# A depthwise convolution as column-tiled tap steps on shifted copies, layer norm beside gate blocks, and earlier w_out loads, in one decoder layer

## The chip, the cores and the metric

The kernel runs on all 8 cores of one Trainium2 chip as one program. The time is the device time of the slowest core in microseconds (us). Some executions fall in a second, slower state: the cores of one die (cores 0 to 3, or 4 to 7) show a lower granted TensorE clock and the time is some per cent longer. The profile of a run shows one execution and, where no core is named, its slowest core. In the views of this document PE is TensorE matmul, PEld its weight load, DVE VectorE, ACT ScalarE, POOL GpSimd and SP SyncE; "SPq" is the queue on which SyncE issues DMA transfers. Every operation passes through one helper, so all lines read L212 and a group is told by its tiles and its form.

## The reference, cut to what matters

The reference is one layer of a decoder. The change touches its middle: a gated linear unit (GLU), a 31-tap depthwise convolution over 1024 channels, a layer norm over the channels, two sigmoid gates, and the product with `w_out`. Attention runs before it and a SwiGLU feed-forward network (FFN) after it; neither is changed.

```python
def conv_branch(u, u_past, w_dw, b_dw, ln_g, ln_b, w_pw, b_pw):
    uc = jnp.concatenate([u_past, u], axis=1)
    y = lax.conv_general_dilated(uc, w_dw[:, None, :], window_strides=(1,), padding='VALID', ...,
                                 feature_group_count=D_CONV) + b_dw      # D_CONV = 1024, 31 taps
    y = jax.nn.silu(layer_norm(y, ln_g, ln_b))
    return y @ w_pw + b_pw, uc[:, -(CONV_WIDTH - 1):]

# in decoder_layer:
    glu = z[..., :o1] + b_glu
    u = glu[..., :D_CONV] * jax.nn.sigmoid(glu[..., D_CONV:])
    gate_conv = jax.nn.sigmoid(z[..., o4:o5])
    gate_attn = jax.nn.sigmoid(z[..., o5:])
    conv_out, new_conv = conv_branch(u, u_past, ...)
    attn_out = o_att.reshape(N, L, ATT_OUT) @ w_o_att
    x = x + (gate_conv * conv_out + gate_attn * attn_out) @ w_out
    # ... FFN
```

Each core holds 1024 prompt rows and 16 sample rows. The 1024 channels are worked in 8 blocks of 128 channels, one per partition.

## The kernel before

The operations are listed in program order for each engine, and a helper adds the semaphore waits that the data needs. So the place of a line in the listing fixes its place on its own engine. The GLU and the convolution of a block follow one another at once. A depthwise convolution becomes a matmul by putting each tap on a diagonal: 31 diagonal 128x128 matrices `dg`, each multiplied with a moving window that is shifted by one column.

```python
for ph in range(4):                              # two channel blocks per weight load
    for n4 in range(2):
        n = 2 * ph + n4; ui = n % 2
        for ti, (c0, nc_) in enumerate(TG3):     # columns 357, 357, 356
            # 16 + 16 matmuls: value half and gate half of the GLU; then
            # ACT: sg = sigmoid(gate half); DVE: ubb[ui] or u2 = (value half + bias) * sg
            ...
            if ti == 0:                          # 31 diagonal weight matrices
                S.op('dve', lambda e: e.tensor_tensor(out=dg[ui], in0=mkap(identb, [[0, 31], [1, 128]]), in1=..., op=ALU.mult))
        S.op('pe', lambda e: e.transpose(out=PS[4][0:46, 0:128], in_=u2[:, 310:356], identity=identf))
        for j in range(31):
            S.op('pe', lambda e: e.matmul(PS[2][:, :], lhsT=dg[ui][:, j, :], rhs=ubb[ui][:, j:j + 512], ...))
            S.op('pe', lambda e: e.matmul(PS[3][:, :], lhsT=dg[ui][:, j, :], rhs=ubb[ui][:, 512 + j:512 + j + 512], ...))
            S.op('pe', lambda e: e.matmul(PS[6][:, 0:16]..., lhsT=dg[ui][:, j, :], rhs=ucb[ui][:, :, j:j + 4], ...))  # samples
        ...
```

The layer norm then sums over the channels with a matrix of ones in fp32, block by block, and VectorE and ScalarE apply it. Only after that come the 48 mix blocks (16 output blocks of 128, three column groups each), and only after those the loads of `w_out`.

```python
for ti, (hf, a, nc_, c0) in enumerate(TGL):      # four column groups of 256 or 264
    for n in range(8):
        S.op('pe', lambda e: e.matmul(PS[b0][:, 0:nc_], lhsT=onesf, rhs=yv, start=(n == 0), stop=(n == 7)))
        S.op('act', lambda e: e.activation(out=ysq[qi][:, 0:nc_], in_=yv, func=AF.Square))
        S.op('pe', lambda e: e.matmul(PS[b1][:, 0:nc_], lhsT=onesf, rhs=ysq[qi][:, 0:nc_], start=(n == 0), stop=(n == 7)))
# mean, rstd, then per group and block: DVE subtract, DVE multiply, ACT Silu -> cT
...
for jh in range(8):
    # per mix block: 16 + 16 gate matmuls, 8 with w_pw, 4 with w_o; ACT: two sigmoids; DVE: three ops -> mixT
    ...
wo = [load_out(c) for c in range(4)]             # w_out in four quarters
for t in range(8):
    S.dma('sp', xacc[t], xext[1024 + 128 * t:1024 + 128 * (t + 1), :])
```

The softmax here doesn't subtract the row's maximum and nothing guards it: scores larger than these inputs give would overflow.

## Time and profile before

The median is 2339.89 us over 4 executions (2337.38 to 2629.14; the longest was slow).

The page of the profile opens with the busy shares, the busy tenths of PE and the granted clock in 40 slices of the span, and the chain of work that ended last, by engine:

```profile
span 2349.9 us, 34317 instructions; the slowest of 8 cores (2316.9 to 2349.9 us)
PE 2138.1 (91%) x13248; PEld 1247.2 (53%) x13248; DVE 816.0 (35%) x1418; ACT 367.5 (16%) x712; POOL 125.2 (5%) x129
...
PE   3697799798899978999958989999999999999997
...
PEclk9898899899999998999989999999999999999987
...
PE 85%; DMA 8%; DVE 3%; ACT 2%; issue 2%; another core or an unknown queue 1%; SPq 0%; DVEq 0%; ACTq 0%; POOLq 0%
```

TensorE bounds the kernel: it is 91% busy and makes up 85% of the chain. Only work taken from PE, or idle time of PE filled, can shorten it. The low digit in the row "PE" (a 5, in the 21st slice) is the wait for `w_out` at about 1210 us.

The stages on core 5, each from the start of its first matmul (read from PE's timeline):

| stage | starts at, us | lasts, us |
|---|---|---|
| GLU, convolution, layer norm statistics | 568.0 | 295.1 |
| layer norm applied, 48 mix blocks | 863.1 | 342.3 |
| product with w_out | 1205.5 | 160.7 |
| FFN, to the end | 1366.1 | 983.8 |

The PE timeline of the kernel before, core 5. The columns are start, duration, engine, line, operation, then the output with the moving input and the weights, the shape of the weights, the shape of the moving input, type and count; in brackets the idle time before it and what ended it.

```profile
617.75 14.72 PE L212 MATMUL ps<-t_55,t_52 128*128 128x357 bf16 x96
634.07 0.27 PE L212 MATMUL ps<-t_43,t_112 128*46 128x128 f32 x1 [1.60 <-DVE t_112 L212]
...
648.68 14.72 PE L212 MATMUL ps<-t_55,t_53 128*128 128x357 bf16 x96
...
834.26 0.68 PE L212 MATMUL ps<-yA,t_45 128*128 128x256 f32 x2
...
882.51 0.45 PE L212 MATMUL ps<-t_120,t_54 128*128 128x347 bf16 x1 [14.52 <-ACT t_120 L212]
...
904.51 4.77 PE L212 MATMUL ps<-t_55,t_52 128*128 128x346 bf16 x16 [6.65 <-ACT t_135 L212]
...
1205.45 3.62 PE L212 MATMUL ps<-wf_146,t_134 128*128 128x512 bf16 x16
1240.82 5.18 PE L212 MATMUL ps<-wf_143,t_134 128*128 128x512 bf16 x16 [31.75 <-DMA wf_143<-w_out]
```

One block is 14.72 us of GLU matmuls, 1.60 us idle for the transpose, and 14.5 us of convolution (from 634.18 to 648.68). The statistics take 28.8 us (834.26 to 863.1). The mix stage then waits for the layer norm, in steps of 14.52 and 6.65 us among others: it lasts 342.3 us, where 48 blocks at 6.49 us are 311.5, so 30.8 us are lost. And the second quarter of `w_out` is 31.75 us late: its load was issued at 1202.2 us only. (The first quarter's, on a free buffer, was issued at 1129.5 us, since the POOL queue runs ahead of PE.)

One more reading matters: the attention stage of this same kernel already uses column tiles (weights of 128 rows by 32 columns). Three of them with different moving inputs start within 10 ns, and the next three begin 0.22 us later (the fourth line):

```profile
115.42 0.39 PE L212 MATMUL ps<-t_52,t_55 128*32 128x512 bf16 x1
115.42 0.39 PE L212 MATMUL ps<-t_53,t_55 128*32 128x512 bf16 x1
115.43 0.39 PE L212 MATMUL ps<-t_54,t_55 128*32 128x512 bf16 x1
115.65 0.38 PE L212 MATMUL ps<-t_52,t_55 128*32 128x512 bf16 x1
```

### The profile page before, as it was taken

The page shows a single profiled execution, that of the slowest core. Times are in us where ns is not written, and L with a number is a line of the kernel's source. Part 1 is how long each engine was busy: PE and PEld are TensorE (multiplying, and loading weights), DVE is VectorE, ACT ScalarE, POOL GpSimd, SP SyncE. Part 2 cuts the span into 40 slices and gives each one's busy share as a digit, 9 for nine tenths or more (in the row PEclk, how much of TensorE's full clock was granted, in tenths as well). Part 3 has the DMA queues.
Part 4 walks back from the last instruction along what each step waited for, and adds up shares of the span by engine and source line. Part 5 has one row for each costly group of instructions (what it writes and reads, how often), then busy time and mean ns, then how long its engine had stood idle before and what let it go on. Part 6 is the DMA issues. An engine that isn't in the chain of part 4 may idle for free.

```text
span 2349.9 us, 34317 instructions; the slowest of 8 cores (2316.9 to 2349.9 us)
## 1 busy us (share of the span) xinstructions
PE 2138.1 (91%) x13248; PEld 1247.2 (53%) x13248; DVE 816.0 (35%) x1418; ACT 367.5 (16%) x712; POOL 125.2 (5%) x129
## 2 busy tenths in 40 slices
PE   3697799798899978999958989999999999999997
PEld 2354354465455554666633555665565565565653
DVE  2543375464222214222211424224324314414125
ACT  3451121111011143111100320000000000000012
POOL 0000000000000100010000010000000000010000
PEclk9898899899999998999989999999999999999987
DMA  8847678756500072555656589987989895554303
GB/s 196 192 94 111 99 174 167 149 149 122 96 1 1 10 93 27 73 79 71 86 128 149 72 151 149 185 126 140 168 127 160 143 148 85 90 79 76 62 21 126
DMA packets 217971, 256.93 MB, mean 109 GB/s; under 512 B 6626, under 2 KB 186082, under 8 KB 212540
## 3 DMA queue, kind: packets, MB, share of 16 engines
q0 software_dynamic: 185808, 127.93, 39.9%
q1 hardware_dynamic: 30468, 82.96, 12.5%
q10 hardware_dynamic: 1536, 43.85, 7.8%
q8 instruction: 108, 1.77, 0.3%
q14 instruction: 51, 0.42, 0.1%
HBM read 366.61 MB, written 60.30 MB: 182 GB/s over the span
## 4 chain that ended last, share of the span: by engine, by line
PE 85%; DMA 8%; DVE 3%; ACT 2%; issue 2%; another core or an unknown queue 1%; SPq 0%; DVEq 0%; ACTq 0%; POOLq 0%
PE ps L212 85%; DMA wf_143<-w_out 2%; DMA t_52<-w_in 1%; DMA t_58<-xext 1%; DMA t_69<-cv 1%; DMA t_67<-sqkv 1%; DMA t_63<-ck 1%; DMA t_64<-ck 1%; DVE t_133 L212 0%; DVE t_132 L212 0%; DMA t_59<-xext 0%; DMA t_105<-state 0%; ACT t_60 L212 0%; ACT t_172 L212 0%
## 5 line engine op out<-in xcount | busy, mean ns | idle before, releaser
L212 PE MATMUL ps<-t_55,t_52 128*128 128x347 bf16 (+3 forms) x1152 | 188.6, 321 | 6.7 <-ACT t_135 L212 6.7
L212 PE MATMUL ps<-t_54,t_55 128*128 128x512 bf16 (+1 forms) x640 | 149.7, 388 | 14.9 <-DMA t_54<-w_in 14.9
L212 PEld LDWEIGHTS ps<-t_55,t_52 128*128 128x128 bf16 x1152 | 115.4, 100 | 70.6 <-issue 7.0
L212 PE MATMUL ps<-t_53,t_55 128*128 128x512 bf16 (+1 forms) x640 | 146.6, 383 | 5.2 <-DVE t_55 L212 5.2
L212 PE MATMUL ps<-t_55,t_53 128*128 128x347 bf16 (+3 forms) x960 | 150.8, 312 | 0.0
L212 PEld LDWEIGHTS ps<-t_55,t_53 128*128 128x128 bf16 x960 | 93.9, 98 | 48.8
L212 PE MATMUL ps<-t_52,t_55 128*128 128x512 bf16 (+1 forms) x432 | 109.1, 411 | 7.0 <-DMA t_52<-w_in 6.9
L212 ACT ACTIVATE t_170<-ps 128x347 f32<-128x347 f32 (+1 forms) x66 | 30.4, 460 | 542.4 <-PE ps L212 542.4
L212 PEld LDWEIGHTS ps<-t_54,t_55 128*128 128x128 bf16 (+1 forms) x640 | 76.0, 122 | 70.6 <-issue 23.7
L212 PEld LDWEIGHTS ps<-t_53,t_55 128*128 128x128 bf16 (+1 forms) x640 | 75.1, 122 | 60.1 <-issue 11.4
L212 PE MATMUL ps<-t_134,wh_152 128*128 128x347 bf16 (+1 forms) x576 | 93.9, 318 | 0.0
L212 PE MATMUL ps<-t_134,wh_151 128*128 128x347 bf16 (+1 forms) x576 | 93.9, 318 | 0.0
L212 PE MATMUL ps<-t_134,wh_153 128*128 128x347 bf16 (+1 forms) x576 | 93.1, 316 | 0.5 <-DVE t_134 L212 0.5
L212 PE MATMUL ps<-t_134,wh_154 128*128 128x347 bf16 (+1 forms) x576 | 90.9, 311 | 0.0
L212 PE MATMUL ps<-t_120,t_54 128*128 128x347 bf16 (+1 forms) x384 | 66.7, 314 | 17.4 <-ACT t_120 L212 17.4
L212 PE MATMUL ps<-t_134,wh_150 128*128 128x347 bf16 (+1 forms) x480 | 77.9, 317 | 0.0
L212 PE MATMUL ps<-t_134,wh_149 128*128 128x347 bf16 (+1 forms) x480 | 77.7, 317 | 0.0
L212 PEld LDWEIGHTS ps<-t_52,t_55 128*128 128x128 bf16 (+1 forms) x432 | 43.6, 105 | 60.6 <-issue 23.8
L212 PE MATMUL ps<-t_134,wh_147 128*128 128x347 bf16 (+1 forms) x480 | 75.7, 311 | 0.0
L212 PE MATMUL ps<-t_134,wh_148 128*128 128x347 bf16 (+1 forms) x480 | 75.7, 311 | 0.0
L212 ACT ACTIVATE t_171<-ps 128x347 f32<-128x347 f32 (+1 forms) x66 | 30.4, 460 | 283.7 <-PE ps L212 283.7
L212 PEld LDWEIGHTS ps<-t_134,wh_151 128*128 128x128 bf16 x576 | 57.4, 100 | 31.0
(379 smaller groups left out, 3079.9 us busy)
## 6 DMA issues: line engine op xcount, KB each, us to landing
t_52<-w_in POOLq DMA_DIRECT2D x12, 1024.0 KB, 10.4
t_53<-w_in POOLq DMA_DIRECT2D x10, 1024.0 KB, 12.5
t_58<-xext SPq DMA_DIRECT2D x8, 1024.0 KB
t_59<-xext SPq DMA_DIRECT2D x8, 1024.0 KB, 7.5
kso<-ck ACTq DMA_DIRECT2D x8, 1016.0 KB, 10.7
vso<-cv ACTq DMA_DIRECT2D x8, 1016.0 KB, 10.9
t_52<-w_in POOLq DMA_DIRECT2D x3, 2048.0 KB, 25.0
wh_153<-w_gate POOLq DMA_DIRECT2D x6, 1024.0 KB, 9.9
```

The lines of the kernel that those rows point to most:

```text
L212: self.q[eng].append(lambda e: getattr(e, meth)(*a, **kw).then_inc(s, 1))
```

## The change

The change has three parts.

1. **Convolution in four column tiles.** A diagonal 128x128 matrix uses one row in 128 for each output. In its place the kernel handles 32 channels per column tile, with the four quarters of the 128 partitions holding the same 32 channels shifted by 0, 8, 16 and 24 columns. One matmul then does four taps for 32 channels, and eight steps `a` do 32 taps (the last is zero). The four tiles `g` work side by side. The price is the shifted data: 16 copies from `ubb` to `U4` for each block, each of 32 partitions and 1032 columns, on the SP queue. The convolution of block n-1 is placed inside block n, after its second column group, so that PE has something to do while the copies run. The sample rows are convolved on VectorE.
2. **Layer norm beside gate blocks.** VectorE and ScalarE add up the values and the squares over the 8 blocks as they come, so that the ones-matmuls are needed once. The sigmoids become tanh, whose results are kept for the first nine gate blocks (`ND = 9`); PE runs those while the layer norm is applied, and the nine mixes are done afterwards.
3. **Two of four w_out loads start in the mix stage**, after blocks 35 and 41.

The diff, cut to its core:

```diff
+        def conv_in(n):
+            i_ = n % 2
+            S.op('dve', lambda e: e.tensor_tensor(out=dgc[i_], ...))          # 32 small diagonals
+            for g in range(4):
+                for i in range(4):
+                    S.dma('sp', U4[i_][32 * i:32 * i + 32, g, :], ubb[i_][32 * g:32 * g + 32, 8 * i:8 * i + 1032])
+
+        def conv(n):
+            i_ = n % 2
+            for hf in range(2):
+                for a in range(8):
+                    for g in range(4):
+                        S.op('pe', lambda e: e.matmul(PS[4 + hf][32 * g:32 * g + 32, :], lhsT=dgc[i_][:, 4 * a + g, :], rhs=U4[i_][:, g, a + 512 * hf:a + 512 * hf + 512], start=(a == 0), stop=(a == 7)))
+                S.op('act', ...)                                               # + bias -> yv[n]
 ...                                             # in block n, after column group ti
-                for j in range(31):
-                    ... three matmuls with dg[ui][:, j, :] ...
+                if ti == 1 and n > 0:
+                    conv(n - 1)
+                    conv_sample(n - 1)
+                    stat_add(n - 1)
+            S.op('act', lambda e: e.copy(out=ubb[ui][:, 714:1054], in_=u2[:, 0:340]))
+            conv_in(n)
+            ...
+            if n4 == 1:
+                if ph < 2:
+                    glu_load(ph + 2)             # weights of a later pair of blocks, on the POOL queue
+                else:
+                    gates_load(ph - 2)
 ...
-        a4_load(0)
-        a4_load(1)
-        ... statistics, layer norm, then the mix ...
+        gates_load(1)
+        gate(0)
+        rows_out(7)
+        gate(1)
+        conv(7)
+        ...
+        gate(2)
+        stat_mm(6, 0, 0, 512)
+        ...                                      # ln_rstd, ln_apply between gate(3) ... gate(8)
+        for it in range(48):
+            if it >= ND:
+                gate(it)
+            mix(it)
+            ...
+            if it == 35:
+                wo.append(load_out(0))
+            if it == 41:
+                wo.append(load_out(1))
 ...
-        wo = [load_out(c) for c in range(4)]
+        wo += [load_out(2), load_out(3)]
```

## The prediction

> **What bounds it now.** TensorE: 85% of the chain of waits, 91% busy, at a granted clock of 1.00 in every long stretch. The change touches 568 to 1241 us (PE timeline):
>
> - GLU and convolution, 568 to 834 us. One channel block: 14.7 us of GLU matmuls, 1.6 us idle for a transpose waiting on VectorE, 14.5 us of convolution (31 taps x 0.460 us). The first block also waits 9.6 us (state load, sample normalisation).
> - Layer norm, 834 to 905 us: 28.8 us of fp32 ones-matmuls, then about 30 us more than the mix needs, while ScalarE and VectorE normalise.
> - Mix, 48 blocks of 6.49 us, all PE. Then PE waits 31.8 us for a w_out load issued only at 1202 us; the next 16 matmuls take 5.2 instead of 3.6 us (cold clock).
>
> **Removed.** A convolution becomes 8 taps x 2 halves, each four 128x32 column tiles. This trace already has such tiles: three of 512 columns start together every 0.215 us, four of 256 every 0.108 us. That agrees with the Trainium skill, "TensorEngine Tiling (Array Packing)", Key Properties: tiles work in parallel. So 16 x 0.216 = 3.5 us instead of 14.5, and the 1.6 us bubble goes: 12.6 x 8 = 101 us. First block: 8 us. Statistics: 2080 fp32 columns x 1.69 ns = 3.5 instead of 28.8 us: 25 us. Layer norm beside nine gate blocks (9 x 4.7 = 42 us of PE; VectorE needs about 22 us to apply, 10 for statistics): 30 us. First two w_out loads 39 us and more before use (a load lands in 27): 32 us. Ideal sum, all PE: 196 us.
>
> **Given back.**
> 1. Each block needs 16 copies on the SP queue. SP issues one per about 0.5 us (eight xacc loads took 4.5 us), so 8 us, after 2 us of evacuation and before some 2.5 us of landing: 12.5 us after the GLU ends, while PE reaches the convolution after 9.8 us. PE stalls 2 to 5 us per block, most beside weight loads: 28 us. The clock may drop after such stalls (the skill, "TensorE: Matmul & The Clock Gate", gives about 3.4 us of idleness; here 2.9 us was enough).
> 2. The second pair of gate weights is loaded twice: four 1 MB transfers of about 10.5 us, ahead of w_pw and w_o; gate block 6 needs them after about 36 us. Stall 5 to 10 us.
> 3. Nine mixes alone (1.8 us PE, about 1.7 us VectorE each): 3 us.
>
> 196 - 28 - 8 - 3 = about 157 to 160 us.
>
> **Predicted: 2180 us, range 2140 to 2222.** Faster by over 2%: 0.96; within 2%: 0.03; slower: 0.01.
>
> **What shows it.** Right: 64 matmuls of 128x32 per block, in groups of four every 0.216 us, 3.5 us per block; PE idle before them, ended by the shifted copies, 2 to 5 us each; idle at gate block 6, ended by w_in; no idle before the first w_out matmul; ones-matmuls 3.5 us; mix blocks 6.49 us. Wrong: column tiles in series (14 us per block); table reloads between tanh and silu making ScalarE late; mixes held by the layer norm; a wait for the residual rows (xacc) in place of w_out's.
>
> **What would make it wrong.** Copies issued faster than 0.5 us each (then 2145), or slowed by weight loads so that each stall also costs clock (then 2215); tiles with different moving data not overlapping (above 2250).

## The result and the profile after

The changed kernel takes 2204.45 us in the median of 4 executions (2200.43 to 2290.21; the longest was slow). The ratio to the kernel before is 0.9422, with a 95% interval of 0.9403 to 0.9441. A ratio here is the mean time of one kernel's fast runs over that of the other's fast runs of the same rounds, so it is not quite the ratio of the medians quoted. The outputs are correct. The saving is 135.4 us; 157 to 160 were predicted.

The page of the profile after, with the lines that answer to those shown of before:

```profile
span 2204.4 us, 33953 instructions; the slowest of 8 cores (2170.5 to 2204.4 us)
PE 2020.9 (92%) x12900; PEld 1183.2 (54%) x12900; DVE 806.4 (37%) x1416; ACT 384.1 (17%) x719; POOL 127.5 (6%) x131
...
PE   3797699879987889999999899999999999999996
...
PEclk9898899989998899999999999999999999999999
...
PE 84%; DMA 7%; SPq 2%; DVE 2%; issue 2%; ACT 1%; another core or an unknown queue 1%; DVEq 0%; ACTq 0%; POOLq 0%
```

The hole of the 21st slice is gone. New is "SPq 2%" in the chain: the queue that issues the copies has come onto the critical path.

| stage, core 5 | before, us | after, us | saved, us |
|---|---|---|---|
| first GLU matmul to first gate matmul | 295.1 | 206.0 | 89.1 |
| to first w_out matmul | 342.3 | 332.6 | 9.7 |
| to first FFN matmul | 160.7 | 127.1 | 33.6 |
| FFN, to the end | 983.8 | 965.8 | 18.0 |

The last row isn't the work of the change: in the profile before, core 5 took 983.8 us for the FFN and core 4 took 980.5, and the other six took 966.4 to 966.9. On core 0 the three changed stages save 90.3 + 9.4 + 36.5 = 136.2 us, and the FFN 0.8. That agrees with the 135.4 us between the medians. The last convolution has moved from the first stage to the second, so the rows are not a breakdown by cause.

The PE timeline after, core 5, in the same columns. First blocks 1 and 2:

```profile
626.37 5.04 PE L212 MATMUL ps<-t_55,t_53 128*128 128x357 bf16 x32
631.82 0.38 PE L212 MATMUL ps<-t_119,t_107 128*32 128x512 bf16 x1 [0.41 <-DMA t_119<-t_121]
634.28 0.38 PE L212 MATMUL ps<-t_119,t_107 128*32 128x512 bf16 x1 [2.08 <-DMA t_119<-t_121]
636.21 0.58 PE L212 MATMUL ps<-t_119,t_107 128*32 128x512 bf16 x1 [1.56 <-DMA t_119<-t_121]
639.15 5.26 PE L212 MATMUL ps<-t_119,t_107 128*32 128x512 bf16 x61 [2.35 <-DMA t_119<-t_121]
```

`t_119` is one of the two `U4` buffers and `t_121` the `ubb` that it is copied from. The convolution reaches PE before its copies have landed: the first matmul of each of the four tiles waits for its own group, 0.41 + 2.08 + 1.56 + 2.35 = 6.40 us in all. Then 61 matmuls take 5.26 us, where 15 further steps at 0.216 us and one matmul of 0.38 us would be 3.6: the clock has fallen. A matmul takes 0.58 us in place of 0.38.

What SP did at that time (start, duration, engine, operation, output and input, count):

```profile
599.75 9.99 SPq L233 DMA_DIRECT2D t_118<-t_120  x16
623.60 10.26 SPq L233 DMA_DIRECT2D t_119<-t_121  x16
651.43 10.91 SPq L233 DMA_DIRECT2D t_118<-t_120  x16
```

SP needs 10 to 11 us to issue 16 copies, about 0.62 us each (the median from one start to the next). The copies of block 1 are issued until 633.9 us, but PE has been ready for them since 631.4 us. The view of DMA issues gives the size of a copy and the median time from issue to landing:

```profile
t_118<-t_120 SPq DMA_DIRECT2D x64, 64.5 KB, 2.0
t_119<-t_121 SPq DMA_DIRECT2D x64, 64.5 KB, 5.6
```

The even blocks (`t_118`) land after 2.0 us, the odd ones (`t_119`) after 5.6. The difference is the company that they keep: after each odd block the kernel issues 1 MB weight loads on the POOL queue (for block 1 they start at 619.81 and 622.22 us, and the copies at 623.60). Three stretches of core 5 in the view of windows (the header names the columns) are a convolution of an even block, one of an odd block, and plain GLU work:

```profile
core 5: us, PE busy (x) PEld busy (x) DVE busy (x) ACT busy (x) POOL busy (x), PEclk, DMA share, GB/s
607.60:616.60 9.00, 6.04 (x66) 2.68 (x66) 2.34 (x3) 1.25 (x2) 0.00 (x0) 0.81 0.45 156
631.30:644.30 13.00, 6.60 (x65) 2.49 (x64) 3.86 (x4) 1.25 (x2) 0.00 (x0) 0.74 0.93 209
644.40:659.00 14.60, 14.60 (x98) 9.34 (x97) 5.90 (x8) 3.81 (x8) 0.00 (x0) 1.00 0.19 45
```

The convolutions run at a mean clock of 0.81 and 0.74, the GLU at 1.00, and the DMA engines are 93% busy beside the odd block. The waits of PE between 595 and 805 us, core 5 (what was waited for: total us, times, longest) sum up the idle time of all blocks:

```profile
PE ps L212 <- DMA t_119<-t_121: 25.6, 15, 2.4
PE ps L212 <- DMA t_118<-t_120: 13.5, 8, 2.6
```

The rest of the timeline after: statistics, gate blocks 6 and 7, a lone mix, and the start of w_out.

```profile
808.22 1.02 PE L212 MATMUL ps<-t_111,t_45 128*128 128x512 f32 x2
...
827.24 4.88 PE L212 MATMUL ps<-t_55,t_53 128*128 128x347 bf16 x32 [1.19 <-ACT t_149 L212]
832.94 9.60 PE L212 MATMUL ps<-t_55,t_53 128*128 128x347 bf16 x64 [0.82 <-ACT t_151 L212]
842.38 1.34 PE L212 MATMUL ps<-t_129,t_54 128*128 128x347 bf16 x8
...
1111.41 3.62 PE L212 MATMUL ps<-wf_162,t_130 128*128 128x512 bf16 x16
1114.87 3.62 PE L212 MATMUL ps<-wf_159,t_130 128*128 128x512 bf16 x16
```

Gate block 6 waits 1.19 us for ScalarE, not for a weight load, and gate block 7 waits 0.82. The first two quarters of `w_out` follow each other with no gap.

### The profile page after: what moved, and what is told of

Read it like the earlier page. It is cut to its first block, busy times and chain, and to the rows that moved or that the text cites. A ratio compares the mean times of both kernels' runs of the same rounds, so it can differ in the third digit from the quotient of the medians.

```text
span 2204.4 us, 33953 instructions; the slowest of 8 cores (2170.5 to 2204.4 us)
## 1 busy us (share of the span) xinstructions
PE 2020.9 (92%) x12900; PEld 1183.2 (54%) x12900; DVE 806.4 (37%) x1416; ACT 384.1 (17%) x719; POOL 127.5 (6%) x131
## 4 chain that ended last, share of the span: by engine, by line
PE 84%; DMA 7%; SPq 2%; DVE 2%; issue 2%; ACT 1%; another core or an unknown queue 1%; DVEq 0%; ACTq 0%; POOLq 0%
PE ps L212 84%; SPq L233 2%; DMA t_63<-ck 1%; DMA t_52<-w_in 1%; DMA t_58<-xext 1%; DMA t_119<-t_121 1%; DMA t_69<-cv 1%; DMA t_65<-ck 1%; DMA t_118<-t_120 0%; ACT t_188 L212 0%; DMA sqkv<-t_78 0%; ACT t_60 L212 0%; DMA t_59<-xext 0%; DVE xacc_178 L212 0%
## 5 line engine op out<-in xcount | busy, mean ns | idle before, releaser
L212 PE MATMUL ps<-t_55,t_52 128*128 128x347 bf16 (+3 forms) x1152 | 179.1, 315 | 0.0
L212 PE MATMUL ps<-t_55,t_53 128*128 128x347 bf16 (+3 forms) x1152 | 176.7, 312 | 2.0 <-ACT t_149 L212 1.2
L212 PEld LDWEIGHTS ps<-t_55,t_53 128*128 128x128 bf16 x1152 | 112.2, 98 | 62.4 <-issue 4.4
L212 PEld LDWEIGHTS ps<-t_55,t_52 128*128 128x128 bf16 x1152 | 113.0, 99 | 60.9 <-issue 1.7
L212 PE MATMUL ps<-t_130,wh_169 128*128 128x347 bf16 (+1 forms) x576 | 93.3, 316 | 0.5 <-DVE t_130 L212 0.5
L212 PE MATMUL ps<-t_130,wh_170 128*128 128x347 bf16 (+1 forms) x576 | 90.9, 311 | 0.0
L212 PE MATMUL ps<-t_130,wh_168 128*128 128x347 bf16 (+1 forms) x576 | 90.9, 311 | 0.0
L212 PE MATMUL ps<-t_130,wh_167 128*128 128x347 bf16 (+1 forms) x576 | 90.8, 311 | 0.0
L212 PE MATMUL ps<-t_130,wh_165 128*128 128x347 bf16 (+1 forms) x480 | 75.7, 311 | 0.0
L212 PE MATMUL ps<-t_130,wh_164 128*128 128x347 bf16 (+1 forms) x480 | 75.7, 311 | 0.0
L212 PE MATMUL ps<-t_130,wh_166 128*128 128x347 bf16 (+1 forms) x480 | 75.7, 311 | 0.0
L212 PE MATMUL ps<-t_130,wh_163 128*128 128x347 bf16 (+1 forms) x480 | 75.7, 311 | 0.0
L212 DVE TENSOR_TENSOR t_184<-ps,t_187 128x347 bf16<-128x347 f32 (+1 forms) x36 | 18.7, 520 | 151.6 <-PE ps L212 151.6
L212 DVE TENSOR_TENSOR t_184<-ps,t_186 128x347 bf16<-128x347 f32 (+1 forms) x36 | 18.7, 520 | 151.4 <-PE ps L212 151.4
```

Of the source, the lines that this page charges most:

```text
L212: self.q[eng].append(lambda e: getattr(e, meth)(*a, **kw).then_inc(s, 1))
```

## The experiments

The theory (called A in the expectations where they name one): the copies are bound by their issue on SP. PE arrives before they are done, and the short waits cost twice: once as idle time and once as cold clock. The rivals are that the bytes of the copies or the weight loads beside them are the cause, that the column tiles of the convolution run slower than those of the attention stage, and that the time was lost elsewhere, in the double weight load, the layer norm or w_out. All runs gave correct outputs. All edits are to the changed kernel, and "against the change" means the difference of the two ratios to the kernel before, times 2340 us; by the intervals such a difference is good to some 6 us. The kernel before had medians of 2342.75, 2345.83 and 2345.36 us in the three groups of runs. In the runs other than before and after the views call every buffer only `t`.

### late: the convolution at the end of the block

```diff
-                if ti == 1 and n > 0:
-                    conv(n - 1)
-                    conv_sample(n - 1)
-                    stat_add(n - 1)
             ...
             conv_in(n)
             ...
+            if n > 0:
+                conv(n - 1)
+                conv_sample(n - 1)
+                stat_add(n - 1)
```

> One edit: the convolution of a block is recorded one GLU pass later (after all three tiles of the next block and after that block's copies are issued) instead of after the second tile. Theory A (the SP queue issues the 16 copies one after the other, about 10 us a block, and PE comes too early and then runs cold): PE reaches the convolution about 18 us after the block's GLU, the copies are there after 14 us (18 us beside a weight load), so the idle time before convolutions 0 to 6 falls from 31.9 us to under 5 us, their 64 matmuls take 3.5 us instead of 5.3 to 6.5 us, and the whole takes about 2204 - 50 = 2155 us. Rival B (column tiles with different moving data run slower by themselves): idle falls, but the 64 matmuls still take 5.3 us or more, 2170 us or more.

Measured: 2158.47 us, ratio 0.9216 (0.9198 to 0.9235), 48 us below the change. The third column group of the GLU (about 4.9 us) now covers the copies. (The profiled execution took 2185.07 us because cores 6 and 7 spent 990 to 993 us in the FFN; core 5, which is read here, spent 965.7.) The waits on core 5 in the same stretch as above, and a line of its PE timeline, 61 matmuls of block 1:

```profile
PE ps L212 <- DMA t<-t: 7.4, 6, 3.7
PE ps L212 <- ACT t L212: 2.0, 2, 1.5
PE ps L212 <- DVE t L212: 1.2, 2, 0.7
...
637.56 3.62 PE L212 MATMUL ps<-t,t 128*32 128x512 bf16 x61 [0.43 <-DMA t<-t]
```

The 61 matmuls take 3.62 us, where those of the same block took 5.26 in the change. In five of the eight convolutions the last matmul starts 3.29 to 3.30 us after the first, in two 4.19 and 4.42 us after it; groups of four start within 10 ns of each other, every 0.216 us. Only the last convolution, which has no third GLU column group after its copies to cover them, still takes 12.28 us, 6.23 of them idle. So the tiles themselves run as predicted, and the loss was one of timing: 39.1 us of idle time fell to 7.4, and the saving is larger than that fall: in the clock records of core 5 the clock fell to half in each of the eight convolutions of the change, and here in the last alone.

### split32: the same bytes in twice the copies

```diff
-                    S.dma('sp', U4[i_][32 * i:32 * i + 32, g, :], ubb[i_][32 * g:32 * g + 32, 8 * i:8 * i + 1032])
+                    for h in range(2):
+                        S.dma('sp', U4[i_][32 * i:32 * i + 32, g, 516 * h:516 * h + 516], ubb[i_][32 * g:32 * g + 32, 8 * i + 516 * h:8 * i + 516 * h + 516])
```

> One edit: each copy is cut into two halves by columns, so 32 copies a block with the same bytes. Theory A (issue on the SP queue bounds the copies): the copies of a block are issued in about 20 us instead of 10, every convolution comes 8 to 10 us later, whole about 2204 + 70 = 2275 us. Rival C (bytes or DMA bandwidth bound the copies): no more than 10 us longer.

Measured: 2275.21 us, ratio 0.9708 (0.9692 to 0.9724), 67 us above the change. Waits of PE, core 5:

```profile
PE ps L212 <- DMA t<-t: 69.7, 21, 4.6
```

The bytes are the same and the packets are half as long. Twice the issues cost about 8 us more per block, against the 10 us that 16 more issues take. The number of copies decides; a bound by bytes would have left the time alone. The trace says so directly: SP starts a copy every 0.62 us in the median, as in the change, though each copy has half the bytes. (**act** below bears on the same point without changing the packets.)

### hold: weight loads after the copies

After blocks 1, 3 and 5 a POOL operation reads the last column of `U4`, and so waits for all copies, before the weight loads are issued.

```diff
             if n4 == 1:
+                if n < 7:
+                    S.op('pool', lambda e: e.tensor_copy(out=..., in_=U4[ui][:, :, 1031:1032]))
                 if ph < 2:
                     glu_load(ph + 2)
```

> One edit: after blocks 1, 3 and 5 the weight load waits (a small copy on GpSimd reads the last column of the shifted copies) until that block's copies have landed. Theory A with sharing (weight loads that start at the same moment as the copies slow their landing from 2 us to 5.6 us): idle before convolutions 1, 3 and 5 falls from about 6 us to about 3 us each, and they run as the even ones do (9 us instead of 13 from GLU end to convolution end); whole about 10 us shorter, 2194 us. Rival (odd blocks are slower for another reason, such as their own buffers): no change.

Measured: two fast executions at 2200.54 and 2197.73 us and two slow ones. The ratio of fast runs is 0.9389 (0.9370 to 0.9408), 8 us below the change; the two intervals overlap slightly, so the times alone don't show a gain. On core 5 the waits are 32.6 us:

```profile
PE ps L212 <- DMA t<-t: 32.6, 19, 5.6
```

Blocks 1, 3 and 5 now wait as little as the even ones (2.90 to 3.63 us, in place of 5.91 to 6.40), and their copies land after 2.0 us where the trace records it (5.0 to 5.8 in the change), so the weight loads beside the copies do account for the difference between odd and even. Block 2 got worse (5.49 us in place of 4.05). Its recorded landings are 2.0 us too, so the held load did not slow them; SP began its copies some 1.5 us later after the GLU, and why is open. The weight loads are a smaller cause than the issue: even a block without one waits about 3 us.

### act: half of the copies issued by ScalarE

```diff
-                    S.dma('sp', U4[...], ubb[...])
+                    S.dma('sp' if i < 2 else 'act', U4[...], ubb[...])
```

> One edit to the changed kernel: of the 16 copies of a block, 8 are issued on the SP queue and 8 on the ScalarE queue; the convolution stays after the second tile. Theory A (one queue's issue rate is the limit): both halves are issued in about 5 us, so even blocks find their copies landed after about 9.5 us and PE idles under 1 us there, odd blocks (beside a weight load) about 3 us; the idle time of 39 us before the eight convolutions falls to 12 to 18 us, whole about 2204 - 35 = 2170 us. Rival C (the DMA engines or bytes bound the copies): under 8 us gained.

Measured: 2180.14 us in the median, which includes one slow execution; the fast ones are 2175.36, 2184.92 and 2174.23, and the ratio is 0.9277 (0.9249 to 0.9305), 34 us below the change. Same bytes, same packets, same loads beside them: only the issuing engine differs. Waits on core 5:

```profile
PE ps L212 <- DMA t<-t: 13.3, 17, 1.8
```

On core 3, the slowest one of the profiled execution, the convolutions of the even blocks wait 0 to 0.56 us and those of the odd blocks 3.21 to 6.78. With the issue halved, what is left is mainly the slow landing beside the weight loads: on core 5 the copies of the odd blocks land after 5.5 to 7.0 us, those of the even ones after 2.0 to 4.4. The two causes are thus told apart: sharing the issue takes away 34 us, about half of the 65 us that the copies cost (worked out below), and the landing accounts for most of the rest. No run removes both in all blocks; **best** does it in the last block, and there the wait goes.

### nodup: the second load of the same gate weights removed

```diff
-        gates_load(1)
         gate(0)
```

The loop over the blocks has already loaded pair 1 at block 7, so this load is a repetition.

> One edit: the second load of the same pair of gate weights is dropped. As predicted before the run it would cost 5 to 10 us at gate block 6; the trace of the changed kernel shows no wait for w_in there, so now expected: 0 to 4 us shorter, through convolution 7, whose copies then share the DMA engines with one load instead of two.

Measured: 2207.57 us, ratio 0.9426 (0.9411 to 0.9442): no difference from the change. The trace of the change had shown it: the extra transfers are issued at 791.12 and 799.34 us, and no gate block waits for a load.

### gorder: all taps of one tile before the next tile

```diff
-                for a in range(8):
-                    for g in range(4):
+                for g in range(4):
+                    for a in range(8):
```

> One edit to the changed kernel: the two inner loops of the convolution are swapped, so that the eight taps of one column tile stand one after the other and then the next tile (same 64 matmuls). If the gain comes from four tiles working at the same time, a stream in which neighbours use the same tile runs them one after the other: 64 x 0.216 = 13.8 us for a convolution instead of 3.5 (5.3 to 6.5 as it runs now), while the wait for the copies mostly disappears, since the first tile needs four copies only; about +2 to +4 us a block, whole about 2204 + 25 = 2230 us. Rival (the tiles overlap whatever the order): the wait shrinks and the whole gets faster, 2185 us or less.

Measured: 2224.13 us, ratio 0.9465 (0.9442 to 0.9487), 10 us above the change. The time says little: in the profiled execution cores 4 to 7 took 975 to 979 us for the FFN, which this edit doesn't touch, and cores 0 to 3 took 965 to 966, and in all its fast executions some cores of that die show a lower clock. On cores 0 to 3 the way from the first GLU matmul to the first w_out matmul is 3 us longer than in the change (538.8 against 536.1 in the mean). The convolution itself hits neither expectation exactly: it takes 8.77 us from its first to its last matmul start (up to 10.13), where full overlap is 3.3 us and none at all is 13.8. On the other side this order waits less for copies (12.7 us in the same stretch, since the last tile's copies are needed later), so the time hides part of the cost. The starts inside one convolution begin with 0, 226, 442, 660, 876, 881, 1091, 1107, 1310 and 1324 ns: four matmuls alone, then pairs. All 64 take 40 steps of about 0.216 us in place of 16. It fits a PE that starts a matmul of another tile only about four instructions ahead, so that the last four taps of one tile pair with the first four of the next. The trace doesn't name the tile of a matmul, so this is an inference. What is shown is that the order of the loops decides how far the tiles overlap.

### wout and wout2: the w_out load put back

The second quarter of `w_out` waits for the last mix, so that it, and the quarters after it, start late again.

```diff
-            if it == 41:
-                wo.append(load_out(1))
 ...
-        wo += [load_out(2), load_out(3)]
+        S.op('pool', lambda e: e.tensor_copy(out=..., in_=mixT[:, 15, 1039:1040]))
+        wo += [load_out(1), load_out(2), load_out(3)]
```

> One part of the change undone: the load of the second w_out quarter waits for the last mix again, as it did before the change. If the part was worth what the wait of before showed (31.8 us and 1.6 us of cold clock), the whole is about 2204 + 32 = 2236 us, with PE idle about 30 us after the first 16 w_out matmuls. Rival (the wait would have been hidden or have moved to the residual rows anyway): under 10 us.

The first attempt (**wout**) was inconclusive: three of its four executions, the profiled one too, fell in the slow state. The one fast execution took 2262.14 us. The same kernel was run again.

> The same kernel as wout, again, since three of its four executions fell in the slow state: the second quarter of w_out waits for the last mix. Expected as there: about 30 us of PE idle time after the first 16 w_out matmuls, whole about 2204 + 32 = 2236 us (39 us of idle time was seen in a slow execution, so perhaps 2245).

Measured the second time: 2264.78 us, ratio 0.9651 (0.9637 to 0.9665), 54 us above the change; one of the four executions, 2283.12 us, was slow. The PE timeline of core 5 shows the wait:

```profile
1101.04 3.62 PE L212 MATMUL ps<-wf,t 128*128 128x512 bf16 x16
1144.59 5.68 PE L212 MATMUL ps<-wf,t 128*128 128x512 bf16 x13 [39.94 <-DMA wf<-w_out]
```

The wait is 39.9 to 47.1 us on the eight cores, and the matmuls after it run cold. On core 5 the stage lasts 170.0 us in place of 127.1; on core 4, the slowest, it lasts 176.5 in place of 127.1, and the stage before it 336.9 in place of 330.4, which together cover the 54 us. This way of undoing the early load costs more than the kernel before did, because the load starts later: on core 5 it is issued 3.2 us after the first w_out matmul, since it waits for the result of the last mix, and in the kernel before it was issued 3.3 us ahead of it. So the run shows that the early load matters; what it was worth is read from before and after, 31.75 us of wait on core 5 and 23.4 to 34.4 on the eight cores.

### ln and ln2: no gate blocks beside the layer norm

`ND` is 3 in place of 9, so that PE has nothing to do while the layer norm is applied.

```diff
-        ND = 9
+        ND = 3
 ...
-        gate(3)
 ...
-        gate(4)
         ln_apply(0, range(4, 8))
-        gate(5)
-        gates_load(2)
 ...                                             # gate(6), gate(7), gate(8) removed likewise
```

> One part of the change undone: only three gate blocks run before the layer norm instead of nine, so gate blocks 3 to 8 no longer cover it. If covering the layer norm is worth its PE time, the six gates of 4.7 us are lost as cover: about +26 us, 2230 us, with PE idle some 25 us before the first mix. Rival (the tail of the layer norm was never on PE's path after the statistics had shrunk): under 8 us.

Measured: four fast executions of 2240.7, 2235.84, 2249.61 and 2249.57 us; ratio 0.9549 (0.9517 to 0.9581), 30 us above the change. The profiled execution took 4704.4 us (its PE was busy for 4633 us, more than twice as long as in the change).

> The same kernel as ln, for its profile alone, since the profiled execution of ln ran at half speed: about 25 to 30 us of PE idle time between the third gate block and the second mix, ended by ScalarE and VectorE of the layer norm.

It took 2241.19 us. In the PE timeline of core 3 the mix waits for ScalarE, once for 10.19 us and then before nearly every matmul (the first and the last two of those lines):

```profile
832.28 1.32 PE L212 MATMUL ps<-t,t 128*128 128x347 bf16 x4 [10.19 <-ACT t L212]
...
848.04 0.45 PE L212 MATMUL ps<-t,t 128*128 128x347 bf16 x1 [0.98 <-ACT t L212]
849.47 20.77 PE L212 MATMUL ps<-t,t 128*128 128x347 bf16 x131 [0.98 <-ACT t L212]
```

On core 5 the stage from the first gate matmul to w_out lasts 358.4 us in place of 332.6. The gate blocks hide 26 to 30 us, as predicted.

### best: the parts put together

This is **late** and **nodup** together; for the last block alone half of the copies are issued by ScalarE, and the weight load waits for them.

```diff
-                    S.dma('sp', U4[...], ubb[...])
+                    S.dma('act' if n == 7 and i > 1 else 'sp', U4[...], ubb[...])
 ...                                             # conv(n - 1) at the end of the block, as in late
             if n4 == 1:
+                if n == 7:
+                    S.op('pool', lambda e: e.tensor_copy(out=..., in_=U4[ui][:, :, 1031:1032]))
 ...
-        gates_load(1)
         gate(0)
```

> Built on late: the convolution one GLU pass later for blocks 0 to 6, and for block 7, which cannot be put off because the layer norm waits for it, half of the copies on the ScalarE queue, its pair of gate weights loaded once instead of twice, and that load held until the copies have landed. Theory A expects the last 6.2 us of idle time (before convolution 7) and its cold clock to go: under 1.5 us idle there, 64 matmuls in 3.5 us, gate block 6 still not waiting for w_in; whole about 2158 - 9 = 2149 us. If the held load comes too late, gate block 6 waits and the gain is lost.

Measured: ratio 0.9192 (0.9176 to 0.9207), 54 us below the change. The fast executions are 2149.89, 2157.46, 2160.16 and 2151.31 us; two more were slow, and with them the median is 2158.81. Waits on core 5 in the same stretch:

```profile
PE ps L212 <- ACT t L212: 1.8, 2, 1.2
PE ps L212 <- DVE t L212: 1.2, 2, 0.8
PE ps L212 <- DMA t<-t: 0.6, 1, 0.6
```

The last convolution now takes 3.28 us without a wait, in place of 12.28 in **late**. This version beats the kernel before and the changed kernel. Against **late** the interval overlaps slightly, and the two ran in different groups, so its lead over that one is not shown by the times, only by the waits.

## Why the prediction was right, point by point

The time predicted was 2180 us with a range of 2140 to 2222, and 2204.45 us was measured, so the range held; the saving was 22 to 25 us too large. The sum of its terms, in us (measured on core 5):

| term | predicted | measured | where it is read |
|---|---|---|---|
| convolution, all tiles in parallel | 101 | 101 | 16 x 0.216 us, as in **late** and **best** |
| first block | 8 | 9 | GLU of block 0: 33.4 before, 24.6 after, without the 1.6 for the transpose |
| statistics | 25 | 25 | ones-matmuls: 28.8 before, 3.5 after |
| layer norm beside gates | 30 | 29 | 30.8 lost before, 2.0 after; **ln** costs 30 |
| w_out earlier | 32 | 34 | stage: 160.7 before, 127.1 after (26 to 37 on the eight cores) |
| copies | -28 | -65 | 39 idle, 17 cold clock, 9 first matmuls one by one |
| double weight load | -8 | 0 | **nodup** |
| nine mixes alone | -3 | 0 | no waits in 15.9 us (842.38 to 858.30) |
| sum | 157 | 133 | 135.4 between the medians, 136.2 on core 0 |

Each gain that was predicted came within 2 us of its size, and the mechanism was right as well: column tiles that run in parallel, and stalls that the shifted copies end. Two terms were mis-sized.

**The step "PE stalls 2 to 5 us per block, most beside weight loads: 28 us".** It measured 65 us. From the end of a block's GLU work to the end of the convolution the eight blocks take 9.0, 13.0, 11.2, 13.0, 9.0, 13.0, 9.5 and 15.0 us, 92.7 in all, and 8 x 3.46 = 27.7 (3.46 is 16 x 0.216) are left when PE neither waits nor slows: 65 us of loss. Idle time accounts for 39.1 of them. The slow clock accounts for about 17: the last 61 matmuls of a block take 5.26 to 6.50 us in place of 3.62. Most of the last 9 come from the first matmuls of the four tiles, which start one by one as their copies land and not side by side. Three things went into it. First, "SP issues one per about 0.5 us ... so 8 us" was read from the residual loads of another stage; for these copies it is 0.62 us each, so 16 take 10 to 11. Second, the landing was taken as 2.5 us and is 5.6 beside a weight load. Third, and largest, the cold clock was named as a possibility, and even as one of the things that would move the time to 2215, but no term stood for it in the sum, nor for the lost overlap of the first matmuls. The clock fell at each of the eight blocks. **split32** and **act** show that the issue is the largest single cause, **hold** that the weight loads lengthen the landing, and **late** that both kinds of loss go away together once the copies are covered.

**The step "Stall 5 to 10 us" at gate block 6 for the double weight load.** It measured 0. The loads were on the same queue, but the block that needed them came late enough. **nodup** changes nothing.

The two errors partly cancelled each other, which was luck: 37 us too small for the copies, and 11 too large for the double load and the mixes. Without the second, the prediction would have been about 2169 us and 35 us too low in place of 24.

The other parts that the prediction said would show it right did so: groups of four matmuls every 0.216 us (when the clock is up), ones-matmuls of 3.5 us in all, and no idle time before the first w_out matmul. "3.5 us per block" was not seen in the changed kernel, because it ran its convolutions cold; it was seen in **late**. Of the signs that it would be wrong, only ScalarE was late, by 2.0 us at two gate blocks. ScalarE made three table loads from the GLU to w_out, one fewer than before, and none between tanh and silu.

Two places of the Trainium skill bear on this. "TensorE: Matmul & The Clock Gate", Part 1, says the slow clock, half of the full one, is the default and comes back after an idle window of about 3.4 us; its rule further on is to leave no idle gap of more than about 3 us. The size of the drop agrees: cold groups of four came every 422 to 431 ns, about twice 216. The threshold doesn't agree with this trace: on core 5 no gap before a matmul in the eight convolutions was longer than 2.6 us, and still the clock fell in each, for 3.4 us in three of them, 6.8 in four and 10.2 in the last. (The 2.9 us that the prediction calls enough are no clean case: in the trace before, 1.1 us of matmuls of one to four columns follow that gap before the clock falls.) What these blocks have is several gaps in a row, with one or a few matmuls of one quarter of the array between them. "DMA: Bandwidth & Descriptors", section "Issuing engines are not separate DMA queues", says that issuing on several engines "will only save the time on the sequencer it takes to initiate the DMA, which is usually small relative to the DMA itself". Here it was not small: 0.62 us per copy against a landing of 2.0 us, and 10 us for 16, whose issues follow one another while their landings overlap. Sharing it between two engines saved 34 us.

## What to carry to other kernels

When a change turns one large operand into many small transfers, multiply their number by the time of one issue on that queue, and place the consumer where other work covers that sum and the landing; moving three lines was worth 48 us here. Short waits of TensorE that come in a row can cost more than their length: here 39 us of them cost 65, since the clock fell and the tiles did not start together. Where column tiles should run side by side, step through the tiles in the inner loop.

## What the Trainium skill lacked or had wrong

- No page states, for this chip and in microseconds, the time of one issue on a queue; what comes nearest is a count of sequencer cycles for unnamed earlier chips, in the part on a newer one of "DMA: Bandwidth & Descriptors". SP took about 0.62 us for each copy of 64.5 KB (16 in 9.91 to 10.91 us), and the same for copies of half the size. The page calls this time usually small; here sharing it took away about half of what the copies cost.
- The same page's "Anatomy of one DMA" gives a fixed cost of about 2.0 us for the GpSimd path, and calls it constant. These copies went out from SP, for which it gives no such sum; their quiet landing was as long (2.0 us in the median), but beside 1 MB weight loads it was 5.6 us.
- "TensorE: Matmul & The Clock Gate" warns of single idle gaps of more than about 3 us, and where it tells of frequent short ones it gives no length. Here the clock fell to half (422 to 431 ns per group of four, against 216) beside gaps of 2.6 us at most (core 5), several in a row and with few matmuls between them.
- "TensorEngine Tiling (Array Packing)", Key Properties, says that tiles work in parallel, and this agrees (four every 0.216 us). It doesn't say that the order of issue matters: with the tiles in the outer loop a convolution took 8.77 us in place of 3.3.
